# Block 2's input projection as sixteen Strassen units, its gates and convolution kept in DRAM, its recurrence placed beside the gate units, weight sums on VectorE

## The chip, the cores and the metric

One core of a Trainium2 chip runs the whole program. The metric is the device time of one execution in microseconds, median over runs. The profile is of one further execution on the same core; its own time stands beside its span below.

## The reference, cut to what matters

Two blocks follow each other on x of 1024 tokens by 1024 channels, all in float32. The change is in the hand-over between them, in block 2's first half, and in how every Strassen product of the kernel prepares its weights.

```python
# block 1, end
h = rms_norm(x, norm_ffn)
x = x + jnp.square(jax.nn.relu(h @ w_ff1)) @ w_ff2     # w_ff1: 1024 x 4096
x = rms_norm(x, norm_final)
# block 2
proj = x @ w_in + b_in                                 # 1024 x 4096, split 512,512,512,512,1024,1024
u, h, c_gate, b_gate, gate_a, gate_b = split(proj)
g = gelu(s5_ssm(u, ...))                               # complex diagonal recurrence over the tokens
y_a = (g * sigmoid(g @ glu_w + glu_b)) @ w_ssm_out
z = causal_depthwise_conv(c_gate * h, conv_w)          # 3 taps
y_b = (b_gate * z) @ w_conv_out
merged = sigmoid(gate_a) * y_a + sigmoid(gate_b) * y_b
x = layer_norm(ALPHA * x + merged @ w_o, ln1_g, ln1_b)
x = layer_norm(ALPHA * x + (silu(x @ w_gate) * (x @ w_up)) @ w_down, ln2_g, ln2_b)
```

## The kernel before

Every large product keeps float32 accuracy by splitting each operand into a high part (a rounded copy, made on ACT) and a low part (the difference, made on DVE or POOL; both by `split`, L352 and L353) and adding three matmuls of 128x512: high by high, high by low, low by high. Activations lie with channels on the partitions, tokens in two halves of 512.

There are two ways to make a product. `unit` and `mm` (L1334) make 128 output columns for both halves of the tokens from 8 tiles of 128 input channels, 2 x 8 x 3 = 48 matmuls. `sunit` makes 256 output columns by one Strassen level: seven products (`sprod`, L1385) of 4 x 3 matmuls, 84 where the direct way takes 96. `Forms` prepares the seven combinations of the activations (b11, b21, t2, t1, t3, b22, t4), each a high and a low part. `sunit` prepares those of the weights: it splits two quarters directly, builds the sums s1 to s4 from the four quarters and splits these and the last quarter. It yields after its first two products (b11, b21), and then makes the other five in the order t2, t1, t3, b22, t4. Here is how it makes its sums and what has to wait for a copy (L1416 to L1440):

```python
        G.tensor_tensor(s1, r21, r22, op=add)
        G.tensor_tensor(s2, s1, r11, op=sub)
        ...
        self.sprod(Z, w, f["t1"], True)
        p5 = self.tmp("acc")
        A.activation(p5, Z, AF.Copy)
        ...
        self.sprod(Z, w, f["b22"], False)
```

So b22's product adds onto Z only after ACT has copied Z to p5, and t4's adds onto X only after DVE has added X to p5.

Before the change 38 products are `sunit`s: 16 in block 1's first feed-forward product (`ffn1`) and 22 in block 2's gate and up projections. Block 2's input projection, W = `in_w_in_2` with 4096 columns, is 32 direct units (L1334, from yh and yl), 1536 matmuls. Its inputs y are the normalised activations: `Rms` takes squares and column sums per half of the tokens, `rms_tail` runs block 1's last group of w_ff2 products half by half with that, and `fin` (L79) multiplies by gain and norm factor and splits the result, on DVE and POOL in turn.

Block 2 then runs four units for u, twelve conv units (three per tile of 128 channels), with one step of the recurrence (`s5(n)`: `stA`, `stB`, `stC` on quarters of four groups) behind each, the four glu units, and the merge, in which 16 gate units (sigmoid on ACT, kept in SBUF) stand between the products with w_conv_out and w_ssm_out. The recurrence reads u and writes its result transposed through DRAM (`ud`, `gd`); `stC`'s copy out of PSUM (go, L1900) applies gelu, and `glu` reads it back (g) and splits it (gh L1932 on ACT, gl L1933 on DVE).

PE's order is the program's. The other engines' orders come from a scheduler by priority and readiness; each of them works through its own strictly in order, and a wait holds back all that stands behind it. `K.late(ins)` keeps an instruction in program order. DMAs are issued by SP, in order. Weights pass through rings of tiles: wr 3, ws 4, wh and wl 5 each.

## Time and profile before

| | us |
|---|---|
| median of 3 runs (2828.72 to 2835.36) | 2833.05 |
| profiled execution | 2832.16 |
| span of its instructions | 2830.4 |
| PE busy | 2649.6 (94%) |
| DVE busy | 1576.1 (56%) |
| POOL busy | 1074.6 (38%) |
| ACT busy | 1006.6 (36%) |

Busy PE time is a sum of modelled matmul durations. In a row of matmuls the listed 0.39 us of each overlaps the next; the distance between starts tells the pace. The mean granted clock of the profiled execution was 0.96 of full speed.

### The profile page before, as it was taken

The page shows a single profiled execution, that of the slowest core. Times are in us where ns is not written, and L with a number is a line of the kernel's source. Part 1 is how long each engine was busy: PE and PEld are TensorE (multiplying, and loading weights), DVE is VectorE, ACT ScalarE, POOL GpSimd, SP SyncE. Part 2 cuts the span into 40 slices and gives each one's busy share as a digit, 9 for nine tenths or more (in the row PEclk, how much of TensorE's full clock was granted, in tenths as well). Part 3 has the DMA queues.
Part 4 walks back from the last instruction along what each step waited for, and adds up shares of the span by engine and source line. Part 5 has one row for each costly group of instructions (what it writes and reads, how often), then busy time and mean ns, then how long its engine had stood idle before and what let it go on. Part 6 is the DMA issues. An engine that isn't in the chain of part 4 may idle for free.

```text
span 2830.4 us, 39715 instructions
## 1 busy us (share of the span) xinstructions
PE 2649.6 (94%) x15096; PEld 2126.8 (75%) x15096; DVE 1576.1 (56%) x2601; ACT 1006.6 (36%) x1664; POOL 1074.6 (38%) x1017
## 2 busy tenths in 40 slices
PE   7777899799899999999999999999999999999997
PEld 4555676566687888888787888888877888888885
DVE  7899648865585545855454344111587434445346
ACT  4544443433264444312124224122244333342212
POOL 5765334432215432089804332222343333322220
PEclk9888999899999999999999999999989999999998
DMA  3332132222234334545435352111422222233211
GB/s 100 88 89 72 39 121 77 77 90 72 62 94 130 101 119 145 181 143 170 135 89 190 106 144 75 49 49 49 138 71 64 86 89 75 89 121 130 90 49 60
DMA packets 297119, 277.19 MB, mean 98 GB/s; under 512 B 26240, under 2 KB 248576, under 8 KB 296672
## 3 DMA queue, kind: packets, MB, share of 16 engines
q1 hardware_dynamic: 296928, 274.66, 31.2%
q8 instruction: 118, 1.93, 0.3%
q14 instruction: 73, 0.60, 0.1%
HBM read 210.23 MB, written 64.10 MB: 97 GB/s over the span
## 4 chain that ended last, share of the span: by engine, by line
PE 75%; DVE 17%; issue 3%; DMA 2%; ACT 2%; POOL 1%; SPq 0%; ACTq 0%; POOLq 0%; DVEq 0%
PE mm L1334 38%; PE mm L1385 25%; PE mm L645 5%; DVE h L993 2%; DVE stp L991 2%; PE wu L809 2%; DVE cy L798 1%; DVE fbgkq L798 1%; DVE xl L433 1%; DVE res L249 1%; PE ob L809 1%; PE gram L809 1%; PE cp L809 1%; PE mm L227 1%; DMA ca<-rd 0%
## 5 line engine op out<-in xcount | busy, mean ns | idle before, releaser
L353 POOL TENSOR_TENSOR wl<-wr,wh 128x512 fp32r<-128x512 f32 (+1 forms) x261 | 352.6, 1352 | 871.9 <-ACT wh L352 781.9
L352 ACT ACTIVATE wh<-wr 128x512 fp32r<-128x512 f32 (+1 forms) x410 | 250.8, 614 | 747.7 <-PE mm L1334 396.2
L1385 PE MATMUL mm<-t,wh 128*128 128x512 f32 x1216 | 380.4, 394 | 14.8 <-DVE t L353 12.8
L1334 PE MATMUL mm<-fh,wh 128*128 128x512 f32 x816 | 320.8, 393 | 2.3 <-DVE res L1535 2.2
L1334 PE MATMUL mm<-fl,wh 128*128 128x512 f32 x816 | 318.3, 390 | 0.0
L1334 PE MATMUL mm<-fh,wl 128*128 128x512 f32 x816 | 318.2, 390 | 0.0
L1385 PEld LDWEIGHTS mm<-t,wh 128*128 128x128 f32 x1216 | 230.6, 190 | 67.0 <-DVE t L353 16.1
L1385 PE MATMUL mm<-b,wh 128*128 128x512 f32 x848 | 262.8, 391 | 0.0
L1385 PE MATMUL mm<-t,wl 128*128 128x512 f32 x608 | 238.9, 393 | 0.0
L1334 PE MATMUL mm<-yh,wh 128*128 128x512 f32 x512 | 201.7, 394 | 0.0
L1334 PE MATMUL mm<-yl,wh 128*128 128x512 f32 x512 | 200.1, 391 | 1.0 <-DVE yl L353 1.0
L1334 PE MATMUL mm<-yh,wl 128*128 128x512 f32 x512 | 199.8, 390 | 0.0
L645 PE MATMUL mm<-xh,wh 128*128 128x512 f32 (+1 forms) x400 | 173.4, 434 | 24.4 <-ACT rows L860 7.1
L353 DVE TENSOR_TENSOR wl<-wr,wh 128x512 fp32r<-128x512 f32 x149 | 109.3, 734 | 150.4 <-ACT wh L352 150.4
L1385 PEld LDWEIGHTS mm<-b,wh 128*128 128x128 f32 x848 | 159.8, 189 | 34.0 <-issue 0.5
L1416 POOL TENSOR_TENSOR ws<-wr 128x512 f32<-128x512 f32 x38 | 65.1, 1712 | 316.3 <-DVE wl L353 216.3
L1334 PEld LDWEIGHTS mm<-fh,wh 128*128 128x128 f32 x816 | 153.4, 188 | 37.4 <-DVE res L1535 3.0
L1334 PEld LDWEIGHTS mm<-fh,wl 128*128 128x128 f32 x816 | 153.5, 188 | 32.2
L1334 PEld LDWEIGHTS mm<-fl,wh 128*128 128x128 f32 x816 | 153.5, 188 | 32.2 <-issue 0.7
L645 PE MATMUL mm<-xl,wh 128*128 128x512 f32 (+1 forms) x400 | 171.2, 428 | 4.1 <-DVE xl L433 4.0
L353 DVE TENSOR_TENSOR wl<-ws,wh 128x512 fp32r<-128x512 f32 x152 | 112.8, 744 | 103.8 <-ACT wh L352 103.7
L645 PE MATMUL mm<-xh,wl 128*128 128x512 f32 (+1 forms) x400 | 169.7, 424 | 0.0
(509 smaller groups left out, 5433.4 us busy)
## 6 DMA issues: line engine op xcount, KB each, us to landing
wr<-in_w_in SPq DMA_DIRECT2D x112, 256.0 KB
wr<-in_w_ff SPq DMA_DIRECT2D x82, 256.0 KB
wr<-in_w_ff SPq DMA_DIRECT2D x32, 512.0 KB
fl<-ffd SPq DMA_DIRECT2D x32, 512.0 KB
wr<-in_w_gate SPq DMA_DIRECT2D x22, 512.0 KB
wr<-in_w_up SPq DMA_DIRECT2D x22, 512.0 KB
fl<-hd SPq DMA_DIRECT2D x22, 512.0 KB
wr<-in_w_down SPq DMA_DIRECT2D x40, 256.0 KB
```

Of the source, the lines that this page charges most:

```text
L227: K.T.matmul(st[:, e * n + k:e * n + k + 1], x[:, k * P:(k + 1) * P], K.ones[:, 0:1], start=e + i + k == 0, stop=i == 1, skip_group_check= ...
L249: K.V.tensor_tensor(r, r, self.rb, op=ALU.mult)
L352: self.A.activation(hi, src, AF.Copy)
L353: (lo_eng or self.V).tensor_tensor(lo, src, hi.bitcast(F32), op=ALU.subtract)
L645: self.T.matmul(ps, a[:, t, :], b[:, sl], start=(first and j == 0), stop=(last and j == 2))
L798: V.scalar_tensor_tensor(y[:, a:b], raw[:, a + o:b + o], cw[:, k:k + 1], y[:, a:b], op0=ALU.mult, op1=ALU.add)
L809: self.T.matmul(out(s), lhsT(s), rhs(s), start=start, stop=stop)
L991: V.tensor_tensor(tm, X3[:, :, 0:j, j:j + 1].to_broadcast([P, 2, j, n]), T3[:, :, j:j + 1, m:16].to_broadcast([P, 2, j, n]), op=ALU.mult)
L993: V.tensor_tensor(T3[:, :, 0:j, m:16], T3[:, :, 0:j, m:16], tm, op=ALU.subtract)
L1334: self.T.matmul(ps, a, b[:, sl], start=(start and k + j == 0), stop=(stop and k == n - 1 and j == 2))
L1385: self.T.matmul(ps, a[:, k, :], b, start=(start and k + j == 0), stop=(k == 3 and j == 2), skip_group_check=True)
L1416: G.tensor_tensor(s1, r21, r22, op=add)
```

## The change

- Block 2's input projection becomes 16 `sunit`s on `Forms` of the residual times the gain, without the norm factor. `norm` multiplies each of the four output quarters of a unit by the factor R (DVE). The normalised activations for the later residual (yd) are made beside units 0 to 7 and stored.
- `ending` (squares, column sums, first forms, the first two t2 steps) and `begin` (first halves of the leading units, the broadcast of R) are made of what `ffn1` had in line, and serve `ffn1` and the new projection. Six units run their first halves ahead where five did, the broadcast stands after four first halves where it stood after three, and the t1, t3, b22 and t4 forms stay in program order on DVE.
- The gates' sigmoids go to DRAM (ga, gb), the convolution's results too (zd). The unit order is u, u, conv, three gate units, five conv units, five gate units. The recurrence runs beside the last five, with one set of buffers; gelu moves from go to the re-read g, 1024 wide. zd is read back and split in the last unit. The merge loads its gates, and the first two conv_out units stand before glu.
- The sums s1 to s4, the split of the last weight quarter, and every weight split that took POOL by default, run on DVE.

```diff
@@ class Forms, split
+        if late:
+            K.late(ins)
@@ rest: t1, t3, b22, t4
-            self.split("t1", j, raw[j][0], j)
+            self.split("t1", j, raw[j][0], j, True)
...
@@ wts
-            hi, lo = self.piece(wap, r0 + k * P, c0, m, eng or self.G, cols)
+            hi, lo = self.piece(wap, r0 + k * P, c0, m, eng or self.V, cols)
@@ sunit
-        G.tensor_tensor(s1, r21, r22, op=add)
-        G.tensor_tensor(s2, s1, r11, op=sub)
+        V.tensor_tensor(s1, r21, r22, op=add)
+        V.tensor_tensor(s2, s1, r11, op=sub)
...
-        G.tensor_tensor(s3, r11, r21, op=sub)
+        V.tensor_tensor(s3, r11, r21, op=sub)
...
-        G.tensor_tensor(s4, r12, s2, op=sub)
+        V.tensor_tensor(s4, r12, s2, op=sub)
...
-        w = self.wsplit(r22, G)
+        w = self.wsplit(r22, V)
@@ begin (new)
+        for k in range(4):
+            go(2)
+            next(us[k])
+        for h in range(2):
+            self.A.activation(R[:, self.HS[h]], self.bcast(dg[h]), AF.Copy)
+        for k in range(4):
+            next(us[k])
+        for k in range(4, ahead):
+            next(us[k])
+            next(us[k])
+            go(2)
@@ block2
+        def norm(m, h, src):
+
+            t = src if (m, h) != (1, 0) else self.tmp("t")
+            V.tensor_tensor(t, src, R[:, self.HS[h]], op=M_)
+            return t
...
+        def gates(e, p):
+            def ev(m, h, src):
+                d, t = 2 * p + m, norm(m, h, src)
+                A.activation(t, t, AF.Sigmoid, bias=self.vec("b_in", 16 + 8 * e + d))
+                dma(gt[e][d][:, self.HS[h]], t)
+            return W, 2048 + 1024 * e + p * 2 * P, ev
...
-            A.activation(go[:, 4 * (q % 2):4 * (q % 2) + 4, :], yp, AF.Gelu_apprx_tanh)
+            A.activation(go[:, 4 * (q % 2):4 * (q % 2) + 4, :], yp, AF.Copy)
...
-        self.head([u(0), u(1)], N1)
-        self.unit(u(2))
-        self.unit(u(3))
-        for i in range(12):
-            self.mark("conv")
-            self.unit(conv(i))
-            s5(i)
+        gs = [gates(e, p) for e in range(2) for p in range(4)]
+        cs = [conv(p, k) for p in range(2) for k in range(3)]
+        us = self.begin([u(0), u(1), cs[0]] + gs[:3] + cs[1:] + gs[3:], F, rest, sums, w0, R, dg)
+        side = s5()
+        for i, x in enumerate(us):
+            if i == 11:
+                tables(0)
+            for k, _ in enumerate(x):
+                if i > 10 and k in (1, 2, 4):
+                    next(side, 0)
+                if i == 15 and k == 1:
+                    bz = self.load(zd, 0)
+                if i == 15 and k == 3:
+                    self.unpack(bz)
...
             dma(g, gd[c].rearrange("p s k -> p (s k)"))
+            A.activation(g, g, AF.Gelu_apprx_tanh)
...
+        gate_load(0)
+        gate_load(1)
...
+        conv_out(0)
+        conv_out(1)
         for ct in range(4):
             self.unit(glu(ct))
```

On DVE, in the middle of `ffn1`, one unit's second half stood like this before (wl is a low part of a weight, of a quarter wr or of a sum ws; acc and t are the output quarters, L1490 scales them):

```order
L353 TENSOR_TENSOR wl<-wr,wh 128x512 x2
L1431 TENSOR_TENSOR acc<-acc,mm 128x512
L353 TENSOR_TENSOR wl<-ws,wh 128x512
L1490 SCALAR_TENSOR_TENSOR acc<-acc,R 128x512
L1437 TENSOR_TENSOR acc<-acc,mm 128x512
L353 TENSOR_TENSOR wl<-ws,wh 128x512
L1490 SCALAR_TENSOR_TENSOR acc<-acc,R 128x512
L1490 SCALAR_TENSOR_TENSOR t<-mm,R 128x512
L353 TENSOR_TENSOR wl<-ws,wh 128x512 x2
```

and on DVE at the same place now:

```order
L319 TENSOR_TENSOR wl<-ws,wh 128x512
L1358 TENSOR_TENSOR ws<-wr 128x512
L319 TENSOR_TENSOR wl<-ws,wh 128x512
L1359 TENSOR_TENSOR ws<-ws,wr 128x512
L1374 TENSOR_TENSOR acc<-acc,mm 128x512
L319 TENSOR_TENSOR wl<-ws,wh 128x512
L1493 SCALAR_TENSOR_TENSOR acc<-acc,R 128x512
L1371 TENSOR_TENSOR ws<-wr 128x512
L1380 TENSOR_TENSOR acc<-acc,mm 128x512
L319 TENSOR_TENSOR wl<-ws,wh 128x512
L1493 SCALAR_TENSOR_TENSOR acc<-acc,R 128x512
L1377 TENSOR_TENSOR ws<-wr,ws 128x512
```

The four sums (L1358, L1359, L1371, L1377) have come between the splits and the adds; the adds (L1374, L1380) still wait for PE, and what stands behind them with them.

On DVE at the start of `ffn1`, the forms of the activations stood like this before (t1_, t2_, t4_ are low parts of forms, cb and ts what they are made from, qy and qt the norm's root, dg its diagonal, t_7411 a unit's first quarter):

```order
L110 SCALAR_TENSOR_TENSOR t1_7550<-ts_7377,vecs_63,t1_7550 128x512
L154 SCALAR_TENSOR_TENSOR cb_7638<-res_5368,vecs_63,ts_7377 128x512
L346 SCALAR_TENSOR_TENSOR qt_7347<-qt_7347,qa_7345 128x8
L353 TENSOR_TENSOR wl_7514<-wr_7512,wh_7513 128x512
L353 TENSOR_TENSOR t2_7382<-ts_7377,t2_7382 128x512
L347 SCALAR_TENSOR_TENSOR qy_7346<-qt_7347,qy_7346 128x8
L1409 TENSOR_TENSOR t_7411<-t_7411,mm_7398 128x512
L125 TENSOR_TENSOR ts_7426<-res_5365 128x512
L1304 TENSOR_TENSOR dg_7360<-ident_65,qy_7346 128x512
L1304 TENSOR_TENSOR dg_7362<-ident_65,qy_7346 128x512
```

and on DVE now, at the last of the four t2:

```order
L1351 TENSOR_TENSOR t_7369<-t_7369,mm_7356 128x512
L72 SCALAR_TENSOR_TENSOR t1_7409<-ts_7109,vecs_63,t1_7409 128x512
L72 SCALAR_TENSOR_TENSOR t1_7412<-ts_7199,vecs_63,t1_7412 128x512
L72 SCALAR_TENSOR_TENSOR t1_7415<-ts_7339,vecs_63,t1_7415 128x512
L72 SCALAR_TENSOR_TENSOR t1_7418<-ts_7347,vecs_63,t1_7418 128x512
L312 SCALAR_TENSOR_TENSOR qt_7381<-qt_7381,qa_7379 128x8
L319 TENSOR_TENSOR wl_7537<-wr_7535,wh_7536 128x512
L319 TENSOR_TENSOR t2_7352<-ts_7347,t2_7352 128x512
L319 TENSOR_TENSOR wl_7543<-wr_7541,wh_7542 128x512
L313 SCALAR_TENSOR_TENSOR qy_7380<-qt_7381,qy_7380 128x8
L1351 TENSOR_TENSOR t_7447<-t_7447,mm_7434 128x512
L105 SCALAR_TENSOR_TENSOR cb_7462<-res_5364,neg_6944,acc_7111 128x512
```

Before, the first t2 was split behind the first unit's add and the t1 and t4 steps; now the fourth is, and the t3, b22 and t4 steps stand behind all four.

On ACT, the last conv units and the start of glu before (gh is the high part of g, ch and cz belong to the convolution, bzh is its high part):

```order
L1900 ACTIVATE go_14854<-mm_14845 128x512
L1932 ACTIVATE gh_15014<-g_15012 128x1024
L352 ACTIVATE wh_15081<-wr_15080 128x512
L352 ACTIVATE wh_15125<-wr_15124 128x512
L1827 ACTIVATE cz_14920<-ch_14811,vecs_63 128x1024
L1900 ACTIVATE go_14854<-mm_14924 128x512
L1932 ACTIVATE gh_15020<-g_15018 128x1024
L352 ACTIVATE bzh_14979<-cz_14920 128x512
L352 ACTIVATE wh_15169<-wr_15168 128x512
L1932 ACTIVATE gh_15032<-g_15030 128x1024
```

and on ACT now, in the last unit of the projection (g and gh of the first three quarters; L1363 is the unit's copy u2 and L1368 its copy p5):

```order
L1931 ACTIVATE g_16430<-g_16430 128x1024
L1820 ACT_TABLE_LOAD
L1820 ACTIVATE t_16201<-t_16201,vecs_63 128x512
L1931 ACT_TABLE_LOAD
L1931 ACTIVATE g_16437<-g_16437 128x1024
L1931 ACTIVATE g_16444<-g_16444 128x1024
L318 ACTIVATE wh_16467<-wr_16466 128x512
L1363 ACTIVATE acc_16288<-mm_16187 128x512
L1933 ACTIVATE gh_16433<-g_16430 128x1024
L1933 ACTIVATE gh_16440<-g_16437 128x1024
L1933 ACTIVATE gh_16447<-g_16444 128x1024
L1368 ACTIVATE acc_16307<-mm_16294 128x512
```

Three gelus with their table loads now stand ahead of the unit's copy u2, and three gh between u2 and p5.

## Rows read from the trace of the kernel before

**Rows 1.** The page: busy time of PE, and the chain that ended last.

```profile
PE 2649.6 (94%) x15096; PEld 2126.8 (75%) x15096; DVE 1576.1 (56%) x2601; ACT 1006.6 (36%) x1664; POOL 1074.6 (38%) x1017
PE 75%; DVE 17%; issue 3%; DMA 2%; ACT 2%; POOL 1%; SPq 0%; ACTq 0%; POOLq 0%; DVEq 0%
PE mm L1334 38%; PE mm L1385 25%; PE mm L645 5%; DVE h L993 2%; DVE stp L991 2%; PE wu L809 2%; DVE cy L798 1%; DVE fbgkq L798 1%; DVE xl L433 1%; DVE res L249 1%; PE ob L809 1%; PE gram L809 1%; PE cp L809 1%; PE mm L227 1%; DMA ca<-rd 0%
```

**Rows 2.** Windows: stretch in us, its length, each engine's busy time (instructions), granted clock.

```profile
core 0: us, PE busy (x) PEld busy (x) DVE busy (x) ACT busy (x) POOL busy (x), PEclk, DMA share, GB/s
900.00:950.00 50.00, 50.00 (x222) 41.39 (x221) 23.00 (x34) 21.70 (x37) 20.34 (x14) 1.00 0.33 111
815.00:845.00 30.00, 30.00 (x130) 23.93 (x130) 27.73 (x50) 15.81 (x29) 8.76 (x4) 0.94 0.30 91
845.00:865.00 20.00, 13.73 (x47) 10.31 (x46) 17.21 (x18) 9.51 (x17) 11.46 (x8) 0.74 0.44 145
1503.00:1526.00 23.00, 17.99 (x70) 13.98 (x69) 17.14 (x32) 9.59 (x14) 7.00 (x7) 0.85 0.60 217
2100.00:2150.00 50.00, 44.30 (x186) 35.35 (x184) 48.02 (x81) 31.66 (x54) 14.19 (x8) 0.90 0.16 48
```

**Rows 3.** Waits of PE, 815 to 870 and 1480 to 1530 us: total, times, longest.

```profile
PE mm L1385 <- DVE t L353: 6.3, 2, 3.3
PE mm L1299 <- DVE acc L63: 4.0, 1, 4.0
```

**Rows 4.** Groups by line, 900 to 1100 us: busy us, mean ns | idle before.

```profile
L353 DVE TENSOR_TENSOR wl<-ws,wh 128x512 fp32r<-128x512 f32 x44 | 30.4, 692 | 23.7 <-ACT wh L352 23.6
L1416 POOL TENSOR_TENSOR ws<-wr 128x512 f32<-128x512 f32 x11 | 17.7, 1614 | 82.5 <-DVE wl L353 78.1 <-DMA wr<-in_w_ff 4.4
```

**Rows 5.** Groups by line on PE, 777 to 870 us, then 1440 to 1530 us.

```profile
L2200 PE MATMUL mm<-ones,t 128*128 128x1 f32 x64 | 7.5, 246 | 0.0
L1311 PE MATMUL mm<-dg,ones 128*128 128x512 f32 x4 | 1.9, 592 | 0.0
L1299 PE MATMUL mm<-ones,acc 128*128 128x1 f32 x16 | 2.8, 297 | 4.0 <-DVE acc L63 4.0
L1311 PE MATMUL mm<-t,ones 128*128 128x512 f32 x4 | 2.0, 591 | 0.0
```

**Rows 6.** Groups by line on DVE, recurrence, 1550 to 1720 us.

```profile
L1872 DVE TENSOR_TENSOR ww<-t,mm 128x512 f32<-128x512 f32 x8 | 5.5, 689 | 19.1 <-PE mm L1864 18.4
L1877 DVE TENSOR_TENSOR_SCAN zx<-r,ww 128x128 f32<-128x128 f32 x32 | 10.9, 397 | 0.0
```

**Rows 7.** Timeline of ACT, DVE and PE before glu: start, us, instruction [idle before].

```profile
1709.40 1.15 ACT L1827 ACTIVATE cz<-ch,vecs 128x1024 f32<-128x1024 f32 x1 [0.39 <-DVE ch L1822]
1710.46 0.58 ACT L1900 ACTIVATE go<-mm 128x512 f32<-128x512 f32 x1
1720.62 2.05 ACT L1932 ACTIVATE gh<-g 128x1024 fp32r<-128x1024 f32 x1 [1.70 <-DMA g<-gd]
...
1725.34 0.63 ACT L352 ACTIVATE bzh<-cz 128x512 fp32r<-128x512 f32 x1 [2.15 <-DVE cz L1834]
1725.99 1.28 ACT L1945 ACT_TABLE_LOAD   x1
1727.29 0.69 ACT L1945 ACTIVATE t<-mm,vecs 128x512 f32<-128x512 f32 x1
...
1722.70 1.95 DVE L1933 TENSOR_TENSOR gl<-g,gh 128x1024 fp32r<-128x1024 f32 x1 [1.86 <-ACT gh L1932]
...
1724.71 0.50 PE L1334 MATMUL mm<-gl,wh 128*128 128x512 f32 x1 [1.24 <-DVE gl L1933]
```

**Rows 8.** Groups by line, 2050 to 2175 us, same shape on DVE, and POOL's splits.

```profile
L204 DVE TENSOR_TENSOR acc<-acc,t 128x512 f32<-128x512 f32 x12 | 13.2, 1122 | 0.0
L249 DVE TENSOR_TENSOR res<-res,mm 128x512 f32<-128x512 f32 x16 | 9.7, 677 | 1.5 <-PE mm L1311 1.5
L353 POOL TENSOR_TENSOR wl<-wr,wh 128x512 fp32r<-128x512 f32 x14 | 25.4, 1816 | 52.6 <-ACT wh L352 52.6
```

More of the change, by code (lines that the diff above doesn't have):

```diff
@@ L147, in rest @@
         for j in range(4):
[L148 removed]
+            self.split("b22", j, q[j][1][1], j + 4, True)
             if j % 2:
@@ L1484, in ffn1 @@
         R = self.nf.tile([P, S], F32, name="R")
+        dg = [self.nf.tile([P, HF], F32, name=f"dg{h}") for h in range(2)]
         def up(u):
@@ L1540, in ffn1 @@
             for d in range(KD):
-                down(g, d, (0, 1))
+                for add in down(g, d):
+                    add()
                 next(side, 0)
@@ L1937, in block2, with gate_load, conv_out, ev @@
         yg = []
+        gsl = [(14, 15), (12, 13), (X + 8, X + 9), (X + 10, X + 11), (X + 12, X + 13), (X, X + 1), (X + 8, X + 9), (X + 10, X + 11)]
+        gts = []
+        def gate_load(d):
+            gts.append([self.sl(i, "gt") for i in gsl[d]])
+            for e in range(2):
+                dma(gts[d][e], gt[e][d])
+        gate_load(0)
+        gate_load(1)
+        def conv_out(d):
+            def ev(h, ps):
+                sl = self.HS[h]
+                V.tensor_tensor(gts[d][1][:, sl], ps, gts[d][1][:, sl], op=M_)
+            self.unit((I["w_conv_out_2"], d * P, bz, ev))
         def glu(ct):
@@ L2219, in mixers, with tail, add @@
-        return res, F, lambda: sums(3), w0
+            def tail(d):
+                for hh, sl in enumerate(self.HS):
+                    def add():
+                        if hh == 0:
+                            c = slice(d % 2 * P, d % 2 * P + P)
+                            ps = self.mm([tuple(x[:, t, c] for x in w[d // 2]) for t in range(2)], mix[2:], sl)
+                        else:
+                            hi, lo = self.piece(I["w_out"], (6 * P, 2 * P), d * P, 4, self.V)
+                            ps = self.mm([(hi[:, t, :], lo[:, t, :]) for t in range(4)], mix, sl)
+                        self.V.tensor_tensor(res[d][:, sl], ps, res[d][:, sl], op=ALU.add)
+                    yield add
@@ L2221, in build @@
+            rest, sums, w0 = self.ending(tail, F, I["w_ff1"], 0)
+        return res, F, rest, sums, w0
     def build(self):
```

395 lines of the change are left out of this document (147 added, 248 removed).

## The prediction

> **What bounds the kernel now.** I read the page first: PE is busy for 94% of the span, and the chain that ended last runs through PE for 75% and DVE for 17%, with the direct units (L1334) its largest piece and the Strassen products (L1385) the next [rows 1]. So a matmul less is time less, as long as PE is the engine that is late. Then the windows, for what a matmul costs and where PE is not the one that is late. In a steady stretch of `ffn1` 222 matmuls touch 50 us; as each reaches 0.39 us past its start, their distance is 50.39/222 = 0.227 us, at clock 1.00 and with DVE at 23.0 of 50 us, POOL at 20.3 [rows 2]. Against that pace PE loses time where a norm or the forms of a new input are made: 845 to 865 (47 matmuls are 10.7 us, so 9.7 lost), 1503 to 1526, and 2100 to 2150, where DVE is busy 48.0 of 50 us [rows 2]. The waits name the cause: 6.3 us on the low parts of t2 (DVE t L353) and 4.0 us on the squares of norm2 (DVE acc L63) [rows 3]; the rest of the loss is the granted clock, 0.74 and 0.85 of full speed behind those waits [rows 2].
>
> All times below are against the profiled execution, 2832.16 us (span 2830.4, and 1.8 around it). It lies 0.9 us under the median of the runs, 2833.05, so I let the forecast stand for both.
>
> **The projection's products.** Before: 32 units x 48 = 1536 matmuls; now 16 x 84 = 1344. 192 x 0.227 = **-43.6 us**. The stretch that loses them runs at full pace now, and the order shows them gone, so this term has one answer as long as PE stays the bound there.
>
> **The sums and splits on DVE.** In each of the 54 Strassen units five instructions (four sums, one split) come to DVE, 0.69 us each by the DVE split's row, and leave POOL, where one sum took 1.61 [rows 4]. A unit is 84 x 0.227 = 19.1 us of PE. DVE's share of that in `ffn1` was 23.0/50 x 19.1 = 8.8, and becomes 8.8 + 3.5 = 12.3 us, 64%. The new projection has the same count per unit (its `norm` replaces `ffn1`'s scaling). In the last five units the recurrence adds 1.6 quarters per unit, each three instructions of 0.69, four scans of 0.40 and one more of 0.69 to 0.97, about 4.5 us [rows 6]; DVE then has 19.5 of 26 us (19.1 plus 1.6 x 4.3 us of recurrence on PE). PE's queue hides all of it: the rings hold five split weights, and the order shows each sum and split ahead of the adds of the unit before. I take **0**. What is queued behind a waiting add on DVE is the next two splits; PE reaches them one product (12 x 0.227 = 2.7 us) later at the earliest, and sum, copy and split are 0.69 + 0.63 + 0.69 = 2.0 us. If that cover is gone in every unit, one exposed instruction is 54 x 0.69 = 37 us (a rival below).
>
> **Start of `ffn1`.** Now all four t2 low parts are split before any t3, b22 or t4 step, where the first stood behind t1 and t4 steps, and six first halves (6 x 24 matmuls, 32.7 us) cover them. The two waits of 6.3 us and the slow clock behind them go: -9.7 at most. t1 is needed 2.7 us after t2, t3 and b22 as much later each, and they are queued in that order; one short wait may remain. I take **-9.5**, range -9.7 to -6.
>
> **Norm2 and the start of block 2.** Of 1503 to 1526, 60 large matmuls are 13.6 us and ten small ones 2.4 (half of L1299's 2.8 and of L1311's 2.0) [rows 2, 5], so 23.4 - 16.0 = 7.4 us are lost, and that loss goes: the column sums are added step by step and only the last waits, behind the same six first halves. What takes its place is `ffn1`'s kind of start, which between 815 and 845 ran with the clock at 0.94 [rows 2], about 2.9 us of loss; I put that against it: -4.5. The small matmuls grow: 64 of L2200 and 4 of L1311 (7.5 + 1.9) stand for 16 of L1299 and 4 of L1311 (2.8 + 2.0) [rows 5], +4.6. Together **0**, range -3 to +5.
>
> **The recurrence beside the gates.** PE's instructions for it are the same. Its table and u loads now share SP with the result stores, eight of each per pair; with one set of buffers, `stA` of a pair must wait for its u. **+1**, range 0 to 4.
>
> **The last unit and glu.** Here the cover is thin. ACT has, before the last unit's copy u2, three gelus of 1024 columns (1.15 each, by cz, the same shape) and three table loads (1.28), and between u2 and p5 three gh (2.05 each) and a weight copy (0.63) [rows 7], 6.8 us. PE cannot start b22's product before p5; t1's and t3's products are 5.4 us of cover from u2 on, and with u2 itself late by about 2 us I get a wait of 3.6. On DVE a gl (1.95, [rows 7]) that waits for the third gh stands ahead of the add that t4's product waits for: 3.2 more. Behind 6.3 us of waiting PE lost another 3.4 us at the lower clock [rows 2, 3], so 1.7 here: 8.5. Then glu: from go to the end of gl took 1710.46 to 1724.65 = 14.2 us, and PE waited 1.24 for it [rows 7]. Now a gelu and a table load come between, 16.6 us, against two conv_out units and the first nine matmuls of glu, 57 x 0.227 = 12.9: a wait of 3.7, 2.5 more than before, and 1.5 at the lower clock: 4.0. Together **+12.5**. Nothing like this stretch is in the trace, so the bounds are wide: 0, if ACT gets to its gelus early enough in unit 15 that the copies are not held; and +30, if the twelve transfers of 0.52 MB (g, zd, two gates twice) arrive last, 6.3 MB at the 217/0.60 = 362 GB/s that a share of 0.60 stands for [rows 2], 17 us more.
>
> The Trainium skill ("ScalarE: Activation LUTs", "What ACT_TABLE_LOAD costs") speaks against this part: it gives about 2.66 us for each switch of tables, a drain of 1.38 us included. Here the row shows no drain: a copy begins at 1725.34 and lasts 0.63, the load follows 0.02 us behind it and the sigmoid 0.02 us behind the load [rows 7]. By the page the jam would be 3 x 1.38 = 4.1 us longer and the sum 4 us higher, as an estimate; I go by the row.
>
> **Merge.** The gates are gone from it, and with them the cover for glu's last split before w_ssm_out: +1, range 0 to 5 (gate loads that wait on SP for glu's buffers).
>
> **First layer norm and start of the gate and up products.** DVE is the bound there. 14 splits of w_o come to it [rows 8], and 12 sums of three units: 26 x 0.68 = +17.7. But DVE instructions with both inputs in SBUF were slow there, L204's 1.12 us, where those with one input in PSUM, L249's, took 0.68 [rows 8]; added up over all its groups that excess is 17.7 us too, and it stands where POOL works at 1.82 us per split. **0**, range -5 to +5. The Trainium skill ("GPSIMD Engine Reference", "Key points") says why: POOL shares its SBUF interfaces with VectorE and contends with VectorE's instructions that have two SBUF inputs. The two rows agree with it; without it, were the slowness DVE's own, the term would be +17.7 and the sum that much higher.
>
> **Sum.** -43.6 - 9.5 + 0 + 1 + 12.5 + 1 + 0 = -38.6; 2832.2 - 38.6 = **2793.6 us**.
>
> **The rivals.** (a) No jam in the last unit: ACT is only 36% busy [rows 1] and may be early; the first layer norm gains its 5 too. Then 2793.6 - 12.5 - 5 = 2776. Against it stands the order, with gelus and gh ahead of the copies. (b) A larger jam: the transfers are last, or the u loads hold the recurrence. 2793.6 + 17.5 + 3 = 2814. For it: everything that the change sends through DRAM comes back in these 30 us. (c) Slower than before: DVE, in strict order, becomes the pace of the Strassen units, since a sum now waits behind an add that waits for PE, and the weight's copy on ACT waits for the sum. One exposed instruction per unit gives +37, 2831, no change; two (0.69 x 2 x 54 = 75) give 2868. It decides from 38.6/54 = 0.71 us per unit. For it: three of the five instructions stand right behind waiting adds; against it: DVE at 64%, and 2.7 us of cover per product against 2.0. (d) The change doesn't bring its forms earlier (the scheduler's order meets other waits): the start of `ffn1` keeps its 9.7, 2803, inside the range.
>
> **How the numbers follow.** Forecast, 2780 to 2806 with (d) in it: 0.57. Rival (a), 2762 to 2780: 0.16. (b), 2806 to 2822: 0.17. (c): 0.05 for about 2831, 0.05 for 2840 and more. For 8 in 10 I cut the ends of (a) and (b): 2769 to 2817. About 0.2%, 5.7 us, is what a measurement of this kernel can tell from no change: faster is under 2827.4, slower over 2838.7. So faster 0.90, same 0.05, slower 0.05.
>
> **What would show it.** In the changed profile: 192 matmuls of 128x512 fewer and the same 0.227 us pace in `ffn1` and the gate and up products, DVE near 32 of 50 us there; no wait of PE on t2 at the start of `ffn1`; block 2's projection at 19.1 us per unit and its last five at 26; in the last unit waits of PE on ACT's p5 and DVE's add, with the gelus and gh ahead of them, and one on gl at glu; DVE's two-input instructions at 0.68 us where POOL is idle. Waits of PE on wl or ACT's on ws in every unit would make it wrong towards (c); PE waiting on bz or gates towards (b).

## The result, and the profile after

The changed kernel took 2790.88 us (median of 4 runs, 2788.65 to 2792.41), the kernel before 2831.45 beside it: a ratio of 0.9855, 95% interval 0.9838 to 0.9872. The profiled execution took 2792.41 us, its span 2790.5 where it was 2830.4: 39.9 less, where 38.6 was forecast.

The page of the changed kernel, its busy times and the chain that ended last:

```profile
PE 2616.2 (94%) x14952; PEld 2094.8 (75%) x14952; DVE 1861.0 (67%) x3174; ACT 1076.9 (39%) x1779; POOL 576.4 (21%) x671
PE 74%; DVE 17%; issue 3%; DMA 2%; ACT 2%; POOL 1%; SPq 1%; ACTq 0%; DVEq 0%; POOLq 0%
```

Against [rows 1] PE has 144 matmuls fewer: the 192 that the projection saves, and 48 small column sums more. The chain is shared out as before. POOL lost nearly half of its work, DVE took 285 us on.

The windows of the changed kernel, same columns and stretches as [rows 2]:

```profile
845.00:865.00 20.00, 20.00 (x90) 16.23 (x89) 18.48 (x31) 10.43 (x19) 0.00 (x0) 1.00 0.39 120
900.00:950.00 50.00, 50.00 (x222) 41.41 (x221) 32.65 (x52) 21.72 (x37) 0.00 (x0) 1.00 0.36 116
1503.00:1526.00 23.00, 23.00 (x100) 18.31 (x99) 22.61 (x44) 10.99 (x19) 0.00 (x0) 1.00 0.39 114
```

In the steady stretch PE starts the same 222 matmuls at the same clock, with DVE at 32.65 of 50 us where it had 23.0. In 845 to 865, where PE had 47 matmuls at a clock of 0.74, it has 90 at 1.00, with POOL idle. And 1503 to 1526 is now without a gap. At the start of `ffn1` PE waits no more for t2; its only wait from 812 to 880 us is for the diagonal of the norm factor:

```profile
PE mm L1277 <- DVE dg L1270: 1.2, 1, 1.2
```

To see where 39.9 us went I took, for each stage, its duration, and as its loss the sum of the distances between PE's starts above the median distance of the same matmul:

| stage | before | after | loss before | loss after |
|---|---|---|---|---|
| block 1 up to `ffn1` | 808.0 | 806.6 | | |
| `ffn1` | 321.0 | 311.9 | 13.2 | 4.1 |
| w_ff2 products | 365.7 | 371.6 | 6.9 | 9.0 |
| projection to merge | 504.1 | 472.2 | 12.9 | 23.3 |
| w_o, first layer norm | 100.9 | 99.5 | 6.6 | 5.1 |
| gate and up | 445.9 | 443.3 | 21.9 | 19.3 |
| w_down, end | 264.5 | 265.4 | | |

(The new column sums lie in the w_ff2 stage, 4 us of its growth.) Each column is one profiled execution. In five of the kernels below that have the same instructions in gate and up, that stage's loss is 19.8 to 22.5, so up to 3 us of it vary; `ffn1`'s loss stays within 0.6 us in the eight that have the same instructions there. Of the 54 Strassen units, those away from a stage's start and end lose 0.0 each. What is lost in the projection is lost in units 0 to 2 (2.1), in the five with the recurrence (0.8, 1.4, 0.4, 3.9, 7.2) and in glu and merge (7.4).

The waits of PE from 1780 to 1900 us in the changed kernel (total, times, longest):

```profile
PE mm L1327 <- ACT acc L1368: 2.9, 1, 2.9
PE mm L1300 <- ACT gh L1933: 2.9, 1, 2.9
...
PE mm L1300 <- DVE gl L1934: 1.5, 1, 1.5
PE mm L1327 <- DVE acc L1374: 1.4, 1, 1.4
```

Its timeline there, ACT and DVE in the last unit, then both at glu (start, us, instruction, idle before):

```profile
1826.02 1.06 ACT L1931 ACTIVATE g<-g 128x1024 f32<-128x1024 f32 x1 [0.42 <-DMA g<-gd]
1827.10 1.28 ACT L1820 ACT_TABLE_LOAD   x1
1828.39 0.72 ACT L1820 ACTIVATE t<-t,vecs 128x512 f32<-128x512 f32 x1
...
1832.86 0.58 ACT L1363 ACTIVATE acc<-mm 128x512 f32<-128x512 f32 x1
1833.34 5.79 ACT L1933 ACTIVATE gh<-g 128x1024 fp32r<-128x1024 f32 x3
...
1839.54 0.59 ACT L1368 ACTIVATE acc<-mm 128x512 f32<-128x512 f32 x1
...
1839.17 1.98 DVE L1934 TENSOR_TENSOR gl<-g,gh 128x1024 fp32r<-128x1024 f32 x1 [4.75 <-ACT gh L1933]
...
1842.85 2.00 DVE L1934 TENSOR_TENSOR gl<-g,gh 128x1024 fp32r<-128x1024 f32 x1
...
1845.34 0.69 DVE L1374 TENSOR_TENSOR acc<-acc,mm 128x512 f32<-128x512 f32 x1
...
1853.39 0.58 ACT L1886 ACTIVATE go<-mm 128x512 f32<-128x512 f32 x1
...
1865.04 1.06 ACT L1931 ACTIVATE g<-g 128x1024 f32<-128x1024 f32 x1 [5.08 <-DMA g<-gd]
...
1866.53 1.93 ACT L1933 ACTIVATE gh<-g 128x1024 fp32r<-128x1024 f32 x1
...
1868.49 1.93 DVE L1934 TENSOR_TENSOR gl<-g,gh 128x1024 fp32r<-128x1024 f32 x1 [1.14 <-ACT gh L1933]
```

This is the jam that was forecast, in its place: three gh stand between u2 (L1363) and p5 (L1368), and two gl before the add (L1374). At glu the gelu had to wait for the transfer of g.

### The profile page after: what moved, and what is told of

Read it like the earlier page. It is cut to its first block, busy times and chain, and to the rows that moved or that the text cites. A ratio compares the mean times of both kernels' runs of the same rounds, so it can differ in the third digit from the quotient of the medians.

```text
span 2790.5 us, 39625 instructions
## 1 busy us (share of the span) xinstructions
PE 2616.2 (94%) x14952; PEld 2094.8 (75%) x14952; DVE 1861.0 (67%) x3174; ACT 1076.9 (39%) x1779; POOL 576.4 (21%) x671
## 4 chain that ended last, share of the span: by engine, by line
PE 74%; DVE 17%; issue 3%; DMA 2%; ACT 2%; POOL 1%; SPq 1%; ACTq 0%; DVEq 0%; POOLq 0%
PE mm L1327 33%; PE mm L1300 28%; PE mm L611 5%; DVE h L959 2%; DVE stp L957 2%; PE wu L775 2%; DVE cy L764 1%; DVE fbgkq L764 1%; PE ob L775 1%; DVE xl L399 1%; PE mm L193 1%; DVE wl L319 1%; PE cp L775 1%; DVE res L216 1%; PE mm L1432 0%
## 5 line engine op out<-in xcount | busy, mean ns | idle before, releaser
L1327 PE MATMUL mm<-t,wh 128*128 128x512 f32 x1728 | 539.9, 393 | 11.3 <-DVE t L319 4.1
L1327 PEld LDWEIGHTS mm<-t,wh 128*128 128x128 f32 x1728 | 324.3, 188 | 88.5 <-DVE t L319 7.5
L1327 PE MATMUL mm<-b,wh 128*128 128x512 f32 x1232 | 382.5, 392 | 2.9 <-ACT acc L1368 2.9
L319 DVE TENSOR_TENSOR wl<-wr,wh 128x512 fp32r<-128x512 f32 (+1 forms) x311 | 219.4, 706 | 192.8 <-ACT wh L318 192.5
L1327 PE MATMUL mm<-t,wl 128*128 128x512 f32 x864 | 337.2, 390 | 0.0
L1327 PEld LDWEIGHTS mm<-b,wh 128*128 128x128 f32 x1232 | 231.5, 188 | 53.1 <-ACT acc L1368 4.0
L1327 PE MATMUL mm<-b,wl 128*128 128x512 f32 x616 | 240.2, 390 | 0.0
L318 ACT ACTIVATE wh<-ws 128x512 fp32r<-128x512 f32 x216 | 135.3, 630 | 252.8 <-PE mm L1327 232.0
L319 DVE TENSOR_TENSOR wl<-ws,wh 128x512 fp32r<-128x512 f32 x216 | 148.4, 690 | 71.2 <-ACT wh L318 70.8
L1327 PEld LDWEIGHTS mm<-t,wl 128*128 128x128 f32 x864 | 162.8, 188 | 33.7
L319 POOL TENSOR_TENSOR wx<-wr,wx 128x512 fp32r<-128x512 f32 (+1 forms) x8 | 8.6, 1094 | 846.4 <-ACT wx L318 843.4
L319 POOL TENSOR_TENSOR wl<-wr,wh 128x512 fp32r<-128x512 f32 (+1 forms) x75 | 94.3, 1258 | 280.4 <-ACT wh L318 197.8
```

Source lines behind the costliest of these rows:

```text
L318: self.A.activation(hi, src, AF.Copy)
L319: return (lo_eng or self.V).tensor_tensor(lo, src, hi.bitcast(F32), op=ALU.subtract)
L1327: self.T.matmul(ps, a[:, k, :], b, start=(start and k + j == 0), stop=(k == 3 and j == 2), skip_group_check=True)
```

## Experiments: what made the start of `ffn1` faster

The sum came out, but `ffn1`'s gain had two candidates: the forms kept in order with six halves ahead, to which the prediction gave all of it, or POOL, which no longer works beside DVE. All ratios below are to the kernel before, run on the same chip; differences to the changed kernel are by ratio to its 0.9855 where none else is named.

**Sums back on POOL.** The four sums and the split of the last quarter as before the change, all else as after:

```diff
-        V.tensor_tensor(s1, r21, r22, op=add)
-        V.tensor_tensor(s2, s1, r11, op=sub)
+        G.tensor_tensor(s1, r21, r22, op=add)
+        G.tensor_tensor(s2, s1, r11, op=sub)
...
-        w = self.wsplit(r22, V)
+        w = self.wsplit(r22, G)
```

> The changed kernel with the four sums of weights and the split of the last weight quarter of every Strassen unit back on POOL (the other splits stay on DVE). My theory: in the steady units PE is the pace either way, 222 matmuls per 50 us; what moving them brought is the end of DVE's slow two-input instructions where POOL works, so the time is lost again where DVE is the bound: the first layer norm and the start of the gate and up products, where the changed kernel loses 23.7 us of PE and the kernel before lost 27.3, go back by 2 to 4 us; the start of ffn1 keeps its gain of 9 us, since that came from the order of the forms. Total +2 to +6 us over the changed kernel. Rival A: the start of ffn1 was won by freeing DVE of POOL's contention: then it loses 6 to 9 us again, total +9 to +14. Rival B: DVE is now close to being the pace of the units, and without five instructions per unit it is faster: total -3 to -10.

Measured: 2820.89 us, 0.9955 (0.9940 to 0.9970), some 30 us slower than with the sums on DVE. All expectations were too small. The loss is 10.9 in `ffn1` (4.1), 31.5 in the projection without glu (15.9) and 29.8 in gate and up (19.3); steady units still lose 0.0. So neither engine is the pace, and the starts and the last units decide. They lose in two ways. At the start of `ffn1` PE waits for u2's copy on ACT, and ACT had stood behind a weight copy that waited for POOL's sum (waits of 812 to 880 us):

```profile
PE mm L1327 <- ACT acc L1363: 4.6, 1, 4.6
ACT wh L318 <- POOL ws L1359: 4.7, 1, 4.7
```

At the start of gate and up, 2040 to 2200 us, PE, ACT and DVE have no wait on POOL at all; what is slower there is DVE itself, where instructions with two inputs in SBUF take up to 904 ns (L319 b<-res,b), 684 in the changed kernel.

**The old order of the forms.** No `K.late` on t1 to t4, and no step of theirs inside `ending`:

```diff
-        if late:
-            K.late(ins)
...
-            if j in (1, 2):
-                next(rest)
```

> The changed kernel with the old order of the forms: t1, t3, b22 and t4 are not kept in program order, and the first two t2 steps are not started beside the column sums. Six units still run ahead, the sums stay on DVE. My theory: the gain of 9 us at the start of ffn1 came from the t2 forms being ready; here the waits of PE on t2's low parts come back, 4 to 9 us at the start of ffn1, and something like it at the start of block 2's projection, 2 to 9 us; total +6 to +16 us. Rival: the sixth unit ahead, and DVE free of contention, are cover enough: total within 3 us.

Measured: 2810.52 us, 0.9920 (0.9905 to 0.9935), 18 us slower; `ffn1`'s loss was 13.5, and projection to merge took 15.0 us longer. That looks like the prediction's reason, but the wait is another one. PE's waits of that kernel, 812 to 880 us:

```profile
PE mm L1273 <- DVE dg L1266: 9.5, 1, 9.5
```

PE waits for the diagonal of the norm factor, which now stands behind the forms on DVE, and which the new `begin` broadcasts before it lets the halves go on. The old order is bad in the new sequence; this doesn't say that it was what cost the kernel before its 13.2.

**The kernel before, with its sums on DVE, and nothing else.**

```diff
-        G.tensor_tensor(s1, r21, r22, op=add)
+        V.tensor_tensor(s1, r21, r22, op=add)
...
-        w = self.wsplit(r22, G)
+        w = self.wsplit(r22, V)
```

> The kernel before with one part of the change alone: the four sums and the split of the last quarter of each Strassen unit on DVE. Neither new forms order nor DVE sums alone took the loss from the start of ffn1 (sums on POOL: 10.9 us of loss; old forms: 13.5; both parts: 4.1; neither: 13.2). My theory: the same here, the start of ffn1 keeps its loss within 2 us, and the start of the gate and up products loses 4 to 8 us less, as with the old forms in the changed kernel (21.5 against 28.5): total -3 to -9 us against the kernel before. Rival A: steady units slow down, DVE taking more: 0 to +10 us. Rival B: the sums on POOL hurt only in the changed order: within 2 us.

Measured: 2817.12 us, 0.9971 (0.9958 to 0.9984), span 2813.1. The size by the ratio, -8, is in the expected range; the profiled execution is the fastest of its five, so its stages show more. Of the places one was expected, gate and up, whose loss falls from 21.9 to 16.3; the other was not: `ffn1`'s loss falls from 13.2 to 4.8, though its old order is untouched, and PE's waits on t2 there [rows 3] go:

```profile
PE mm L1385 <- DVE t L353: 0.3, 1, 0.3
```

With this run the four corners for `ffn1`'s loss are there: before 13.2; new order alone (sums on POOL) 10.9; sums on DVE alone 4.8; both 4.1. The order, with all else that the change does there, is worth 2.3 or 0.7, the sums 8.4 or 6.8. Over the whole kernel the same edit is worth 8 us here and 30 in the changed kernel; why so much more there, beyond the two ways named above, was not tried.

How the sums do that is seen on DVE's groups by line, 836 to 870 us (busy us, mean ns of one). The kernel before, then two of POOL's sums of the same form and one instruction of DVE in order of time:

```profile
L353 DVE TENSOR_TENSOR wl<-ws,wh 128x512 fp32r<-128x512 f32 x8 | 7.6, 954 | 1.5 <-ACT wh L352 1.5
L353 DVE TENSOR_TENSOR t<-ts,t 128x512 fp32r<-128x512 f32 x3 | 4.2, 1391 | 0.0
L1409 DVE TENSOR_TENSOR t<-t,mm 128x512 f32<-128x512 f32 x3 | 2.0, 676 | 0.0
...
836.16 4.84 POOL L1416 TENSOR_TENSOR ws<-wr 128x512 f32<-128x512 f32 x1 [60.05 <-DMA wr<-in_w_ff]
848.74 1.27 POOL L1416 TENSOR_TENSOR ws<-wr 128x512 f32<-128x512 f32 x1 [2.63 <-DVE cb L154]
...
850.48 1.75 DVE L353 TENSOR_TENSOR t<-ts,t 128x512 fp32r<-128x512 f32 x1
```

The same groups of DVE with the sums on DVE:

```profile
L353 DVE TENSOR_TENSOR wl<-ws,wh 128x512 fp32r<-128x512 f32 x10 | 6.5, 683 | 2.0 <-ACT wh L352 2.0
L353 DVE TENSOR_TENSOR t<-ts,t 128x512 fp32r<-128x512 f32 x2 | 1.4, 682 | 0.0
L1409 DVE TENSOR_TENSOR t<-t,mm 128x512 f32<-128x512 f32 x2 | 1.4, 678 | 0.0
```

The same instruction on the same shapes takes 682 ns where POOL is idle and 1391 in the mean beside POOL's sums, single ones 1.75 us; an add with one input in PSUM (L1409) takes 676 and 678. In the kernel before, the chain of work from 844.9 to 856.8 us, up to the end of PE's second wait on t2, holds no engine's instructions but DVE's, so their length is what PE waited for. POOL pays too: one sum took 4.84 us while DVE worked through a row of instructions of 0.68, two others of that line in this stretch 1.27 and 1.29. ACT then stood behind POOL's sums here as well, a second thing that goes with the sums on DVE:

```profile
ACT wh L352 <- POOL ws L1417: 6.2, 2, 4.5
```

**Needless work on POOL.** The changed kernel, with four adds of 128x128 on POOL behind each sum of `ffn1` and of gate and up, into a tile that is loaded again before the recurrence reads it:

```diff
+    def dummy(self, w):
+
+        for t in range(4):
+            self.G.tensor_tensor(self.swap, w[:, t, :], self.ident, op=ALU.add)
...
+        if wap is not I["w_in_2"]:
+            self.dummy(s1)
...
+        self.dma(self.swap, I["c_swap"])
```

> The changed kernel, sums on DVE, with work added on POOL that nobody needs: behind each sum of ffn1 and of the gate and up products, four additions of 128x128 on POOL that read the sum just made. It tells apart the two ways in which the sums on POOL cost 30 us. Contention: POOL's reads slow DVE's instructions with two SBUF inputs (1.75 us each while POOL worked, in the run with the sums on POOL); then the starts of ffn1 and of the gate and up products lose most of what they lost there (7 and 10 us): total +8 to +17 us. Waiting: ACT and DVE, in order, stood behind a sum that POOL had not finished (4.7 us on one of them); then nothing waits for POOL here: total 0 to +4 us. My theory: both, more of it waiting: +2 to +8 us.

Measured: 2810.45 us, 0.9945 (0.9931 to 0.9959), 25 us slower (20 by the medians), more than any of the expectations. `ffn1` loses 13.8 (4.1), gate and up 27.5 (19.3). First DVE's longest wait on POOL, 812 to 870 us, then its groups, 836 to 870 us:

```profile
DVE ws L1363 <- POOL swap L1332: 3.0, 1, 3.0
...
L319 DVE TENSOR_TENSOR wl<-ws,wh 128x512 fp32r<-128x512 f32 x7 | 6.0, 862 | 0.0
L119 DVE SCALAR_TENSOR_TENSOR cb<-res,vecs,ts 128x512 f32<-128x512 f32 x4 | 3.8, 942 | 0.0
```

The edit also adds waits, since a sum's buffer is freed only when POOL has read it. At the start of `ffn1` DVE waits 3.7 us for POOL in all, and its slower two-input instructions (these 862 and 942 ns, 682 and 745 in the changed kernel) add about as much, 4.5 us by the groups of the two kernels; what is lost there can't be parted between the two. At the start of gate and up it can: from 2040 to 2200 us DVE and ACT have no wait on POOL, and the two-input instructions are slower all the same (2050 to 2175 us):

```profile
L319 DVE TENSOR_TENSOR b<-res,b 128x512 fp32r<-128x512 f32 x12 | 9.8, 854 | 0.0
```

In the changed kernel this group takes 684 ns. So the 8.2 us more in gate and up are contention, but for the 3 us by which that stage varies.

**The default splits back on POOL.** They belong to the direct products (w_o, w_ff2, glu, merge, w_down):

```diff
-            hi, lo = self.piece(wap, r0 + k * P, c0, m, eng or self.V, cols)
+            hi, lo = self.piece(wap, r0 + k * P, c0, m, eng or self.G, cols)
```

> The changed kernel with the default of the weight splits of the direct products back on POOL (w_o, glu, conv_out, ssm_out and the second feed-forward product), the sums of the Strassen units staying on DVE. My theory: in the first layer norm DVE has 14 splits less (9.5 us), but POOL at 1.8 us per split slows DVE's instructions with two SBUF inputs again; the two cancel, as I forecast: the loss at the start of the gate and up products stays at 19 to 22 us, total within 3 us of the changed kernel, everything else the same. Rival A: contention weighs more, since the sums on POOL cost 30 us over all: +4 to +10 us, at the first layer norm. Rival B: DVE's load weighs more: -3 to -8 us.

Measured: 2798.95 us, 0.9881 (0.9866 to 0.9896), 7 us slower: the size of rival A, but only in part its place. The last unit loses 11.9 (7.2), the first layer norm 7.2 (5.1), glu and merge 8.6 (7.4), gate and up 21.0 (19.3); `ffn1`, which has none of these splits, 3.9.

## Experiments: the last unit and glu

**No gelu.** This kernel leaves out the gelu on g, and its table loads with it:

```diff
-            A.activation(g, g, AF.Gelu_apprx_tanh)
```

> The changed kernel without the gelu on g: four activations of 1024 columns and the table loads around them are left out, so its output is not the reference's. My theory of the last unit: ACT is behind there, since gelus and table loads stand ahead of the copy u2, so that the three gh between u2 and p5 end too late. Without the gelus u2 is copied about 3 us earlier and p5 is no longer late: the wait of PE for p5 (3.0 us) goes to below 0.5, the wait for DVE's add (1.6) to below 1, the slow clock behind them (1.8) goes; glu's wait on the last quarter of g (4.8 and 1.7 of slow clock) shrinks by a gelu, 1 to 2.5 us. Total -6 to -10 us. Rival: the waits come from the transfers (g, zd, gates) that land late; then the same waits stay and the total is within 3 us.

Measured: 2790.85 us, 0.9850 (0.9835 to 0.9865): no difference. PE's waits of that kernel, 1780 to 1900 us:

```profile
PE mm L1327 <- DVE acc L1374: 2.9, 1, 2.9
PE mm L1300 <- DVE gl L1933: 1.5, 1, 1.5
PE mm L1327 <- ACT acc L1368: 0.7, 1, 0.7
```

Without gelu p5 comes 2.2 us earlier, but DVE's gl still waits for the third gh, and the add behind it costs what p5 had cost: the last unit loses 7.4 (7.2). Only at glu, where nothing stands behind, 4.2 us go (loss 3.2 where it was 7.4); 2.7 us more are lost in gate and up (22.0 where it was 19.3), a stage with the same instructions, and the rest in small differences elsewhere.

**Three gh on POOL.**

```diff
-            A.activation(nat(hi), perm(g), AF.Copy)
+            if c < 3:
+                G.tensor_copy(nat(hi), perm(g))
+            else:
+                A.activation(nat(hi), perm(g), AF.Copy)
```

> The changed kernel with the first three gh copies (1024 columns, 1.93 us each on ACT) made by POOL, which is idle there; the fourth stays on ACT. My theory: p5's copy no longer stands behind three gh, so PE's wait for it (3.0 us, and the slow clock of 1.8 us behind it) goes; the low parts on DVE still come from gh, so the wait for DVE's add (1.6) may stay or grow by 2 if POOL takes over 3 us for a copy. glu's wait on the last quarter stays at 4 to 5 us. Total -2 to -5 us. Rival: the transfers are what is late: no change, within 2 us. Second rival: POOL's copy takes so long (over 5 us) that glu waits for the first quarters too: +3 to +8 us.

Measured: 2789.91 us, 0.9847 (0.9831 to 0.9864): 2 us better by the ratio, which is within the noise. The jam of the last unit goes (2.1 where it was 7.2), which shows that the gh made it. POOL's three casts take 7.38 us, 2.46 each. But a new wait takes its place at the first conv_out products, on a low part of zd:

```profile
PE mm L1300 <- DVE fl L319: 4.1, 2, 3.3
```

**The gates' loads behind zd's**, with gh on POOL, to see whether zd came late on the queue:

```diff
+                    gate_load(0)
+                    gate_load(1)
...
-        gate_load(0)
-        gate_load(1)
```

> The first three gh copies on POOL, and the loads of the first two pairs of gates (four of 0.52 MB) issued behind those of zd instead of ahead of them. With gh on POOL alone ACT waited 3.7 us for zd to land and conv_out then waited 3.4 us for its low parts. My theory: half of that wait is the transfers' order; zd lands 4 to 6 us earlier, the wait at conv_out goes to 0 to 1.5, and the gates are still in time for the first multiplication; glu may wait 1 to 3 for the last quarter of g, whose stores stand behind the gates now. Total -3 to -6 us against the changed kernel. Rival: the wait is DVE's queue (two gl of 1.98 us ahead of the low parts of zd), and the transfers' order does nothing: within 2 us of the run with gh on POOL alone.

Measured: 2795.47 us, 0.9873 (0.9858 to 0.9888), 5 us slower than the changed kernel. The wait for zd's low parts stays at 4.1 us, so the transfers' order wasn't its cause. Glu waits again for the last gh. ACT's idle time ahead of it was not for g to land: the gelu and its table load stood behind a weight copy that waited for PE.

```profile
PE mm L1300 <- ACT gh L1947: 2.8, 1, 2.8
...
1865.48 0.63 ACT L318 ACTIVATE wh<-wr 128x512 fp32r<-128x512 f32 x1 [4.85 <-PE mm L1300]
...
1867.43 1.06 ACT L1942 ACTIVATE g<-g 128x1024 f32<-128x1024 f32 x1
```

**The recurrence a unit earlier**, without and with gh on POOL, so that g comes before the last unit:

```diff
-        us = self.begin([u(0), u(1), cs[0]] + gs[:3] + cs[1:] + gs[3:], F, rest, sums, w0, R, dg)
+        us = self.begin([u(0), u(1), cs[0], cs[1]] + gs[:2] + cs[2:] + gs[2:], F, rest, sums, w0, R, dg)
...
-            if i == 11:
+            if i == 10:
...
-                if i > 10 and k in (1, 2, 4):
+                if i > 9 and k in (1, 2, 4):
```

> The changed kernel with the recurrence one unit earlier: the order of the units is u, u, conv, conv, two gate units, four conv units, six gate units, and the recurrence starts beside the eleventh unit instead of the twelfth, so that its last piece stands a unit before the end. My theory: the wait at glu (6.5 us with its slow clock) is the chain of the last quarter of g, from go through DRAM and gelu to gl; a unit earlier it is hidden, under 1.5 us. The last unit keeps its loss of about 7 us, or gets up to 4 more, since ACT now has four gelus and four gh there. The recurrence's own waits (about 6 us in its units) stay. Total -2 to -6 us against the changed kernel. Rival: ACT, not the chain, holds glu, and the fourth gelu and gh only make the last unit later by what glu gains: within 2 us.

> The recurrence one unit earlier, and the first three gh copies on POOL. With those copies on POOL alone the last unit lost 2.1 us instead of 7.2, but the first conv_out product then waited 3.4 us for the low parts of zd, which DVE makes behind two gl. My theory: the last unit loses 2 to 4, conv_out 2 to 5 for the same reason, glu's chain under 1.5: total -4 to -8 us against the changed kernel. Rival: DVE has a fixed amount of work to do between the last unit's products and glu (four gl of 1.98 us, eight low parts of zd, the unit's own adds), and whatever is freed on ACT is lost again on DVE: within 3 us.

Measured: 2799.19 us, 0.9886 (0.9871 to 0.9900), and 2803.92, 0.9900 (0.9884 to 0.9917): 9 and 13 us slower, both against expectation. The first kernel's waits of PE, 1770 to 1900 us:

```profile
PE mm L1300 <- ACT fh L318: 5.4, 1, 5.4
...
PE mm L1850 <- DMA ut<-ud: 2.1, 1, 2.1
```

Work on ACT comes together in the same last units, now zd's high parts (fh), and PE waits 2.1 us for u's way back from DRAM. With one more conv unit among the leading six, units 2 and 5 lose 4.7 and 1.9 us at the start, where units 1 and 2 lost 0.8 and 1.3.

## A version put together from these

**Forms kept in order only where there is a gain (the two starts with `begin`), three gh on POOL, their gl late:**

```diff
-        if late:
+        if late and self.gain:
...
-            K.late(ins)
+            if self.gain:
+                K.late(ins)
...
-            A.activation(nat(hi), perm(g), AF.Copy)
-            V.tensor_tensor(nat(lo), perm(g), nat(hi).bitcast(F32), op=Su)
+            if c < 3:
+                G.tensor_copy(nat(hi), perm(g))
+            else:
+                A.activation(nat(hi), perm(g), AF.Copy)
+            ins = V.tensor_tensor(nat(lo), perm(g), nat(hi).bitcast(F32), op=Su)
+            if c < 3:
+                self.late(ins)
```

> Three edits on the changed kernel: the first three gh copies on POOL, their gl kept in program order on DVE (behind the low parts of zd), and the forms kept in program order only where a norm's gain is in them, not for the gate and up products. With gh on POOL alone the last unit lost 2.1 us instead of 7.2 and conv_out lost 4.5; with the order of the forms undone everywhere, the start of the gate and up products with the layer norm ahead of it lost 21.5 instead of 24.4. My theory: the last unit 2, conv_out 0 to 1.5 since DVE makes zd's low parts first, glu 1 to 4, the layer norm's start 21 to 22: total -5 to -9 us against the changed kernel, near 2784. Rival: glu waits for the gl that now stand last, and the start of the gate and up products varies by 3 us from run to run whatever the order: within 3 us.

Measured: 2778.70 us, 0.9837 (0.9822 to 0.9852): faster than the kernel before, and by the ratios 5 us faster than the changed kernel, though the two intervals still overlap. The last unit loses 2.3. What is left is the wait for zd, and DVE's timeline has its cause:

```profile
1848.29 5.68 DVE L1939 TENSOR_TENSOR gl<-g,gh 128x1024 fp32r<-128x1024 f32 x3
1853.89 0.68 DVE L321 TENSOR_TENSOR fl<-fl,fh 128x512 fp32r<-128x512 f32 x1
```

The last low part of zd stands behind three gl. First layer norm, gate and up together lose 20.7 here, and 21.5 in the kernel with the old forms; in six kernels that keep the forms in order there (the changed one and those with no gelu, gh on POOL, gates' loads behind zd, the recurrence earlier) they lose 24.4 to 27.6. The kernel of the next experiment has the old forms there too and loses 24.1, so these 3 us are not clear of the stage's own spread.

**The same, with those gl behind the first conv_out unit:**

```diff
-            ins = V.tensor_tensor(nat(lo), perm(g), nat(hi).bitcast(F32), op=Su)
-            if c < 3:
-                self.late(ins)
...
+        for g, (hi, lo) in zip(g_, gs_):
+            self.late(V.tensor_tensor(nat(lo), perm(g), nat(hi).bitcast(F32), op=Su))
```

> As e9_best, with the low parts of the gates' copies (gl) of the last quarters put behind the low parts of zd that the first convolution products of the merge read. Theory (the merge's first products wait 3.57 us there because the last low part of zd stands behind three gl, 5.68 us in a row on VectorE): that wait falls below 0.5 us, the products of the gates wait 0 to 2 us for the first gl, and the total falls 2 to 4 us against e9_best, a ratio of 0.982 to 0.983 to the kernel before. Rival (VectorE has the same work to do before the gates' products in either order, so their wait takes the place of the other): the total is within 1.5 us of e9_best.

Measured: 2781.57 us, 0.9825 (0.9812 to 0.9839). PE's waits, 1780 to 1900 us:

```profile
PE mm L1302 <- ACT gh L1938: 1.7, 1, 1.7
PE mm L1302 <- DVE gl L1977: 1.5, 1, 1.5
PE mm L1302 <- DVE fl L321: 0.8, 1, 0.8
```

The wait for zd falls from 4.0 us in all to 0.8, but glu waits 3.2 in its place, as the rival had it, and glu and merge lose 5.8 where they lost 6.9. The ratio is 0.0012 lower, the median 2.9 us higher, the intervals overlap: the two can't be told apart. Both lie 0.2 to 0.3% under the changed kernel's ratio; with two kernels on that side I take the gain as likely, not as settled.

## Why the prediction was right, and where it wasn't

**Products, -43.6: right.** The pace is 222 matmuls in 50 us before and after, and the units between start and end lose 0.0.

**Sums and splits on DVE, 0: the step that failed.** The cost is 0 as put: in the steady stretches DVE at 32.65 of 50 us costs PE nothing. What failed is that the term was sized as a cost alone. DVE's instructions were priced at the 692 ns of a steady row [rows 4], and the row of 1122 with POOL beside it [rows 8] was used for the first layer norm only. The same contention stood at the start of `ffn1`, and so did ACT's waits for POOL's sums, which the prediction doesn't have; there sums on DVE alone are worth 8.4 us (the kernel before with that one edit).

**Start of `ffn1`, -9.5 from the new order: right in size (-9.1), wrong in cause.** The step "all four t2 low parts are split before any t3 step, and six first halves cover them" gives 2.3 us at most by the four corners. The wait on t2 that [rows 3] shows was a wait for a queue of slow instructions, not for a badly ordered one. Rival (d), the forms no earlier, would have come true all the same, though not through t2: in the changed kernel with the old forms `ffn1` keeps a loss of 13.5, since the new `begin` needs the order, as the 9.5 us on dg show.

**Norm2 and the start of block 2, 0: about -2.** The loss of 9.0 around it became 2.3, where 2.9 of clock was kept for it; the 4.6 of small matmuls came. The clock there was 1.00, not 0.94.

**The end of w_ff2's groups: not forecast.** The w_ff2 stage's loss grew by 2.1. The chain of waits in the changed kernel there:

```profile
1366.44 5.96 DMA fl<-ffd
...
1377.46 0.69 DVE res L1508
```

A read of `ffd` is late. The stage's loss was 4.8 to 9.0 over all kernels, and 4.8 to 6.9 in seven others with the same code there, none over the 6.9 of the kernel before, so the 2.1 is likely no lasting effect of the change; it was not tried further.

**Recurrence, +1: +3.6.** Within the bounds, though the last five units took 27.5 us each on average where 26 was put; the four units before the last lose 6.5, most of it in unit 14, where the recurrence lost 2.9 before.

**Last unit and glu, +12.5: right, +12.2, with parts that make up for each other.** p5 was awaited for 2.9 us (3.6 forecast, though 6.8 - 5.4 + 2 is 3.4), the add for 1.4 (3.2), and the loss of the last unit was 7.2 (8.5): so 4.3 of waiting where 6.8 was put, and 2.9 behind it, at a clock of 0.86 from 1838 to 1850 us, where 1.7 was put. Glu took 5.0 (4.0): from go to the end of gl it took 17.1 us (16.6). The parts are not independent: without gelu the add took over p5's wait. The prediction added the two waits as if each had its own cause; both have the third gh. That no drain belongs to a table load holds as well: the load at 1827.10 begins 0.02 us behind the gelu's end and the sigmoid stands 0.01 behind the load, so the 2.66 us of the Trainium skill ("ScalarE: Activation LUTs", "What ACT_TABLE_LOAD costs") don't show here.

**Merge, +1: +1.3.**

**First layer norm, gate and up, 0: -4.** The two 17.7s almost cancel, as put; with the 3 us by which gate and up varies, the gain may be as small as 1. The rows that answer to [rows 8], 2050 to 2175 us in the changed kernel:

```profile
L319 DVE TENSOR_TENSOR wl<-ws,wh 128x512 fp32r<-128x512 f32 x20 | 13.6, 686 | 9.0 <-ACT wh L318 9.0
L170 DVE TENSOR_TENSOR acc<-acc,t 128x512 f32<-128x512 f32 x8 | 5.3, 683 | 0.1
```

acc<-acc,t went from 1122 to 683 ns. That is the sentence of the Trainium skill that the prediction weighed ("GPSIMD Engine Reference", "Key points": POOL contends with VectorE's instructions with two SBUF inputs), and the traces bear it out with a size: 1122 against 683 ns here, 1391 against 682 at the start of `ffn1`.

**The rivals.** (a) and (b) fell with the jam's size. (c), DVE as the pace, didn't come: no unit in the steady stretches loses anything. Moving the sums back was the slow side of this change, at +30 us.

The sum by stages: -43.6 - 9.1 + 2.1 - 2 + 3.6 + 12.2 + 1.3 - 4 = -39.5, of the 39.9 measured. Products came as reasoned, and the jam of the last unit in its place, if with sizes that made up for each other. At the start of `ffn1` it was luck: the prediction gave to the order of the forms what the end of contention brought, and both fall in the same stretch.

## What to carry to other kernels

Before a wait on an engine's result is put down to the order of its queue, compare the same instruction in that stretch and in a quiet one: where it takes twice as long, look at what POOL does beside it. Work moved from POOL to DVE can be a gain even if DVE then has more to do: here DVE went from 56% to 67% busy, and its instructions became shorter. And where several waits hang on one late instruction (here the third gh), don't add them: take the instruction out of the queue, and look who is next.
